# A hybrid decoder layer on one core: the weight sum of a Strassen product made by VectorE, and the order of the merge gate's tiles and the output projection's products changed

## The chip, the cores and the metric

The kernel runs on one NeuronCore of a Trainium2 chip. The engines are TensorE (PE: matmuls; PEld: its weight loads), VectorE (DVE), ScalarE (ACT), GpSimd (POOL) and SyncE (SP), each with its own instruction queue, worked off in order; sixteen DMA engines carry the transfers that SP, ScalarE and GpSimd issue. The metric is device time in microseconds, the median of the runs.

## The reference

The layer has 256 positions and a model width of 1024, all in float32. Cut to what matters here:

```python
h = rmsnorm(x, norm_g) * (1 + scale) + shift            # adaLN: scale, shift, gate from c
proj = h @ w_in                                         # 1024 -> 10 blocks of 1024 columns
q, k, v, g_attn, cb, cc, cx, g_conv, m_attn, m_conv = split(proj)
attn = moba_attention(q, k, v, rel_bias)                # one block of 256 keys: causal softmax
y_attn = (attn * silu(g_attn)) @ w_o_attn
y_conv = (cb * conv3(cc * cx) * silu(g_conv)) @ w_o_conv
merged = sigmoid(m_attn) * y_attn + sigmoid(m_conv) * y_conv
out = rmsnorm(x + gate * (merged @ w_out), final_g)
```

In the kernel's names `ga` and `gc` are the SiLU gates, `ma` and `mc` the sigmoid merge gates of the attention and the convolution branch, `oa` and `oc` the branches' projections (w_o_attn, w_o_conv), and `wo` the output projection (w_out).

## The kernel before, in words

**Precision.** A float32 product is made of three matmuls in a faster format: each operand is split into a high part (ScalarE copies it to the format, line 74) and a low part (VectorE subtracts the high part from the operand, line 75), and high × high, high × low and low × high are summed. So each 1 MB unit of weights costs one 128x2048 instruction on ScalarE and one on VectorE. The names end in `h` and `l`: `ma11l` is the low part of merge gate `ma`, column half 1, contraction half 1.

**Tiles.** `tile(blk, n, kh)` (line 623) loads 512 columns by 512 contraction rows, splits them and issues 24 matmuls of 512 columns, twelve for each of two groups of 128 positions. After `kh` = 1 the result goes through a sigmoid into `SA` (`ma`) or is multiplied into `SA` (`oa`).

**Seven products.** `mc` and `oc` are computed by a Strassen scheme (class `Seven`, line 535). The weights of a block are four quarters (r, c), r the contraction half, c the column half, 1 MB each. Seven products of 12 matmuls replace eight. Three of them, p7, p6 and p4, use a running sum of quarters, `self.sum`: (1,2) + (2,2) for p7, then + (1,1) for p6, then + (2,1) for p4. `begin` (line 542) copies (1,2) into it by a transfer from SP's queue and adds (2,2) by a transfer that adds to what is in memory (`add_on`, line 508, issued by GpSimd); p7 and p6 each start the next addition in the same way, once their operand has been read. p5 uses another sum, `self.first`. p2 and p3 load (2,1) and (2,2) by themselves. The left operands of p7, p5, p6 and p3 are combinations of the activations, made by `combos` (line 511). Partial results wait in three PSUM banks A, B and C; `sink` passes the four result quarters on: for `mc` a sigmoid into `SC` (line 616), for `oc` a multiplication into `SC` (line 619).

**What sets the order.** The code is written in program order, and a tile framework schedules it: each engine's order need not be the written one, and waits are placed by it. Buffers limit how far things run ahead: five raw weight buffers, so a load is issued when the low part of an earlier unit has been made; three buffers each for high and low parts, so a split waits for the matmuls of the third unit before it; and one slot named `W2` which holds first the broadcast condition `csb` for the adaLN gate rows, then `mc`'s sum, then `oc`'s sum, then `gf` (the output gate `gb` and `final_g`).

**From the gates to the end.** Lines 635 to 673 write the order: `ga`'s units with mc's p7, p5, p1 and p6 between them, then the `ma` tiles, mc's p2, p4 and p3, the begin of `oc`, its products and the `oa` tiles. Line 678 transposes the output gate's column into a row, which goes to DRAM and comes back broadcast over all partitions as `gb` (lines 682 and 683). `joined(n)` adds SA and SC for column half n, `turned(n)` transposes the merged half into `M` on TensorE, and the output projection `ao` follows: with `o00` and `o01` for columns 0 to 511, with `o10` and `o11` for the rest. The last quarter of the output gate is multiplied into the raw weights of o10 and o11 (line 699). Then come the residual, the final norm and the output.

Of the kernel before, what the change touches and what calls it, by code (L numbers as in the profile page):

```python
# [35 lines left out]
UNIT = {key: i for i, key in enumerate(UNITS)}  # L36
# [3 lines left out]
def layer_kernel(ctx: ExitStack, tc, x, c, vec, wp_all, slab_all, onehot, final_g, out):  # L40
    nc = tc.nc
# [450 lines left out]
    def gated(blk, src, dst, j):  # L492
        g = unit((blk, j), H, tmp("cc", f"{blk}{j}"))
        sg = tmp("y", f"s{blk}{j}")
        nc.scalar.activation(sg, g, AF.Silu)
        nc.vector.tensor_mul(sg, sg, src[:, 2 * j:2 * j + 2, :])
        put(sg, dst, j)

    def rows_tile(blk, n, kh, xs, a):
        raw = load((blk, n, kh), f"w{blk}{n}{kh}").rearrange("p (k n) -> p k n", k=4)  # L500
        hi, lo = split(raw, [P, 4, 512], f"{blk}{n}{kh}")
        for t in range(2):
            rows_mm(a[t], xs, t, hi, lo, 4 * kh, slice(0, 512), kh == 0, kh == 1)

    def pair(blk, n):
        return [bank(f"a{blk}{n}{t}") for t in range(2)]

    def add_on(t, key):
        nc.gpsimd.dma_start(t, wp_all[UNIT[key]], accum_op=ALU.add)  # L509

    def combos(x, name):
        f = raw_tile([P, 2048], "f" + name).rearrange("p (k n) -> p k n", k=KT)
        nc.vector.tensor_add(f, x[:, :, 0:S].bitcast(F32), x[:, :, S:].bitcast(F32))
        out = {}

        def quarter(t, kh):
            return f[:, 4 * kh:4 * kh + 4, t * P:(t + 1) * P]

        def combo(i, op, a, b, tag):
            v = tp.tile([P, 4, P], F32, tag=tag, name=f"v{name}{i}", bufs=2)  # L520
            op(v, a, b)
            dst = homes[i // 3][:, i % 2]
            nc.scalar.activation(dst[:, :, 0:P], v, AF.Copy)
            nc.vector.tensor_sub(dst[:, :, P:], v, dst[:, :, 0:P].bitcast(F32))
            out[i] = dst
            return v

        homes = [big.tile([P, 2, 4, S], F32R, tag=tag, name=f"sx{name}{tag}") for tag in ("V", "BI")]
        v1 = combo(1, nc.vector.tensor_sub, quarter(1, 0), quarter(1, 1), "cx")
        combo(0, nc.vector.tensor_sub, quarter(0, 0), quarter(1, 0), "cc")  # L530
        v2 = combo(3, nc.vector.tensor_sub, v1, quarter(0, 0), "y")
        combo(4, nc.vector.tensor_add, v2, quarter(0, 1), "cx")
        return {3: out[0], 1: out[1], 2: out[3], 4: out[4]}

    class Seven:
# [5 lines left out]

        def begin(self):
            self.sum = big.tile([P, 2048], F32, tag="W2", name=self.blk + "sum")
            nc.sync.dma_start(self.sum, wp_all[UNIT[self.key(1, 2)]])
            add_on(self.sum, self.key(2, 2))

        def begin_first(self):
# [40 lines left out]

        def p6(self):
            self.product(self.b, self.sum, "p6", False, s=2)  # L590
            add_on(self.sum, self.key(2, 1))
            u3 = self.quad("u3")
            nc.vector.tensor_add(u3, self.b, self.q1)
            nc.vector.tensor_sub(self.q7, u3, self.q7)
            nc.vector.tensor_sub(u3, self.c, u3)
            self.sink(1, 1, u3)

        def p2(self):
            self.product(self.a, self.load(2, 1), "p2", False, t=0, kh=1)
            self.sink(0, 0, self.a)  # L600

        def p4(self):
            self.product(self.b, self.sum, "p4", False, t=1, kh=1)
            nc.vector.tensor_add(self.q1, self.b, self.q1)
            self.sink(1, 0, self.q1)
# [6 lines left out]
    def part(x, t, n):  # L612
        return x[:, t, 512 * n:512 * (n + 1)]
# [9 lines left out]
    def tile(blk, n, kh):  # L623
        if kh == 0:
            banks[blk] = pair(blk, n)
        a = banks[blk]
        rows_tile(blk, n, kh, GA if blk == "oa" else H, a)
        if kh and blk == "ma":
            for t in range(2):
                nc.scalar.activation(part(SA, t, n), a[t], AF.Sigmoid)  # L630
        elif kh:
            for t in range(2):
                nc.vector.tensor_mul(part(SA, t, n), part(SA, t, n), a[t])

    mc, oc = Seven("mc", H, to_gate), Seven("oc", GC, to_merge)
# [17 lines left out]
    mc.p6()  # L653
    gated("ga", AT, GA, 3)
    SA = big.tile([P, 2, D], F32, tag="AT", name="SA")
    tile("ma", 0, 0)
    mc.p2()
    mc.p4()
    tile("ma", 0, 1)
    mc.p3()  # L660
    oc.begin()
    oc.sx = combos(GC, "c")
    tile("ma", 1, 0)
    oc.begin_first()
    tile("ma", 1, 1)
    oc.p7()
    tile("oa", 0, 0)
    oc.p5()
    oc.p1()
    tile("oa", 0, 1)  # L670
    oc.p6()
    oc.p2()
    tile("oa", 1, 0)
    oc.p4()
    gf = big.tile([P, 2 * D], F32, tag="W2", name="gf")
    gb, fg = gf[:, 0:D], gf[:, D:]
# [8 lines left out]
    def joined(n, ts=range(2)):  # L685
        for t in ts:
            nc.vector.tensor_add(part(SA, t, n), part(SA, t, n), part(SC, t, n))

    joined(0)
    oc.p3()  # L690
    M = big.tile([P, KT, 512], F32R, tag="H", name="M")
    wo = {}
# [8 lines left out]

    MR = SA

# [159 lines left out]
```

## Time and profile before

| | |
|---|---|
| median of 3 runs | 326.34 us (326.1 to 326.67) |
| the profiled execution's own time | 326.11 us |
| its span, first to last instruction | 324.2 us |
| TensorE busy | 309.9 us, 96% of the span |
| VectorE busy | 261.1 us, 81% |
| ScalarE busy | 199.3 us, 61% |
| mean granted TensorE clock | 0.992 |
| HBM read | 81.87 MB |

A group or timeline row reads: line, engine, operation, written tile <- read tiles, shape, count. In the timeline the first number is the start in us from the span's start, the second the length; brackets give the idle time of the engine just before and what ended it. A row of stages (A:B) gives length, busy time and number of instructions of PE, PEld, DVE, ACT and POOL, the granted clock, the DMA engines' busy share and GB/s. A DMA row ends with KB each and microseconds from issue to landing. SPq, ACTq and POOLq are the engines' queues. Lengths of neighbouring instructions overlap a little, so steps are better read from start to start.

### The profile page before, as it was taken

To read this page: it belongs to the slowest core of one execution; us is meant where nothing else is said; L and a number is where in the kernel's file an instruction comes from. 1 tells how busy PE (TensorE), PEld (TensorE's weight loads), DVE (VectorE), ACT (ScalarE), POOL (GpSimd) and SP (SyncE) were. 2 spreads that over 40 slices of the span, in tenths; PEclk is the share of its full clock that TensorE was granted. 3 is DMA by queue.
4 is the path that set the end of the run, shared out by engine and by line. 5 is a ranking of instruction groups with operands and counts; after the bars stand their busy time and mean duration, and the time that the engine had idled before them with its cause. 6 is when DMAs were issued, how large, how long until landed. Compare 5 with 4: busy or idle time off the path is not lost.

```text
span 324.2 us, 4594 instructions
## 1 busy us (share of the span) xinstructions
PE 309.9 (96%) x1766; PEld 271.6 (84%) x1766; DVE 261.1 (81%) x365; ACT 199.3 (61%) x292; POOL 15.4 (5%) x25
## 2 busy tenths in 40 slices
PE   7899999999999999999999999999989999599992
PEld 6799999888889988988898888888868888377892
DVE  4899995957699899796978978899757673999774
ACT  2655565763697876676778776779568552722430
POOL 3400000000000000110000100101101010000010
PEclk9999999999999999999999999999999999979999
DMA  7999999996664765997454697738999999250003
GB/s 279 416 409 408 407 418 413 400 351 263 253 236 171 241 281 184 355 213 288 129 210 174 162 293 298 162 129 288 257 327 361 359 394 325 87 196 1 0 2 129
DMA packets 15627, 83.23 MB, mean 257 GB/s; under 512 B 1670, under 2 KB 3062, under 8 KB 8182
## 3 DMA queue, kind: packets, MB, share of 16 engines
q1 hardware_dynamic: 12816, 72.49, 57.0%
q0 software_dynamic: 1184, 8.40, 13.1%
q10 hardware_dynamic: 1606, 2.05, 1.9%
q8 instruction: 14, 0.23, 0.3%
q14 instruction: 7, 0.06, 0.0%
HBM read 81.87 MB, written 1.06 MB: 256 GB/s over the span
## 4 chain that ended last, share of the span: by engine, by line
PE 73%; DVE 11%; DMA 9%; ACT 3%; issue 3%; POOL 0%; POOLq 0%; SPq 0%; ACTq 0%; DVEq 0%
PE acc L202 14%; PE agc L346 5%; PE acc L346 5%; PE acx L346 5%; PE acb L346 5%; DMA ocsum<-in_wp_dram 4%; DMA wma<-in_wp_dram 4%; PE aga L346 3%; PE acb L348 2%; PE agc L348 2%; PE acx L348 2%; PE acc L348 2%; PE av L362 2%; PE av L363 2%; PE av L361 2%
## 5 line engine op out<-in xcount | busy, mean ns | idle before, releaser
L509 POOL DMA_DIRECT2D mcsum<-in_wp_dram x3 | 2.6, 881 | 182.9 <-PE pS L413 119.7
L387 DVE CUSTOM_DVE_ANT_0 gate<-gate,wide,vT 128x1024 f32<-128x1024 f32 x8 | 10.2, 1279 | 0.0
L165 DVE CUSTOM_DVE_ANT_0 ada<-ada,wide,msc 128x1024 f32<-128x1024 f32 x7 | 9.4, 1341 | 0.0
L165 DVE CUSTOM_DVE_ANT_0 ada<-ada,wide,vT 128x1024 f32<-128x1024 f32 x7 | 8.9, 1277 | 0.0
L332 ACT ACTIVATE lowcb<-acb 128x256 f32<-128x256 f32 x8 | 3.0, 374 | 6.5 <-PE acb L348 6.5
L75 DVE TENSOR_TENSOR ma11l<-wma,ma11h 128x2048 fp32r<-128x2048 f32 x1 | 2.3, 2293 | 5.7 <-ACT ma11h L74 5.7
L353 ACT ACTIVATE M<-pm 128x512 fp32r<-128x512 f32 x4 | 2.2, 597 | 7.4 <-PE pm L710 7.4
L75 DVE TENSOR_TENSOR ocp4l<-ocsum,ocp4h 128x2048 fp32r<-128x2048 f32 x1 | 2.3, 2292 | 5.5 <-ACT ocp4h L74 5.5
L737 ACT ACTIVATE SQ<-TT 128x512 f32<-128x512 f32 x3 | 1.9, 627 | 7.1 <-DVE TT L732 7.1
L74 ACT ACTIVATE ocp4h<-ocsum 128x2048 fp32r<-128x2048 f32 x1 | 1.9, 1917 | 6.4 <-DMA ocsum<-in_wp_dram 6.4
L380 ACT ACTIVATE V<-av 128x512 f32<-128x512 f32 x4 | 2.4, 598 | 5.1 <-PE av L363 5.1
L75 DVE TENSOR_TENSOR cb0l<-wcb,cb0h 128x2048 fp32r<-128x2048 f32 x1 | 2.3, 2292 | 3.6 <-ACT cb0h L74 3.6
L74 ACT ACTIVATE ma11h<-wma 128x2048 fp32r<-128x2048 f32 x1 | 1.9, 1918 | 4.7 <-DMA wma<-in_wp_dram 4.7
L477 ACT ACTIVATE y<-cc,vT 128x256 f32<-128x256 f32 x8 | 3.9, 504 | 1.4 <-DVE cc L473 1.4
L332 ACT ACTIVATE lowcx<-acx 128x256 f32<-128x256 f32 x8 | 3.0, 376 | 2.9 <-PE acx L348 2.8
L143 PE MATMUL wt<-ones 128*128 128x128 f32 x18 | 3.8, 381 | 1.0 <-DVE ones L131 1.0
L333 DVE TENSOR_TENSOR cc<-acc,lowcc 128x256 f32<-128x256 f32 x8 | 3.4, 421 | 1.7 <-ACT lowcc L332 1.7
L74 ACT ACTIVATE o01h<-wo 128x2048 fp32r<-128x2048 f32 x1 | 1.9, 1917 | 4.3 <-PE ocC L560 4.3
L202 PE MATMUL acc<-hf,slab 128*128 128x256 f32 x16 | 3.9, 386 | 0.7 <-ACT hf L261 0.7
L362 PE MATMUL ama<-ma11l,H 128*128 128x512 f32 x8 | 3.2, 404 | 1.3 <-DVE ma11l L75 1.3
L75 DVE TENSOR_TENSOR oa01l<-woa,oa01h 128x2048 fp32r<-128x2048 f32 x1 | 2.3, 2291 | 2.7 <-ACT oa01h L74 2.7
L403 DVE TENSOR_TENSOR AX<-QK,AX 128x384 fp32r<-128x384 f32 x8 | 4.4, 551 | 0.0
(552 smaller groups left out, 1149.0 us busy)
## 6 DMA issues: line engine op xcount, KB each, us to landing
ada<-in_wp_dram SPq DMA_DIRECT2D x16, 512.0 KB, 10.2
slab<-in_slab_dram SPq DMA_DIRECT2D x16, 512.0 KB, 10.2
wv<-in_wp_dram SPq DMA_DIRECT2D x4, 1024.0 KB, 11.3
wcc<-in_wp_dram SPq DMA_DIRECT2D x4, 1024.0 KB, 4.8
wcx<-in_wp_dram SPq DMA_DIRECT2D x4, 1024.0 KB, 5.0
gate<-in_wp_dram SPq DMA_DIRECT2D x4, 1024.0 KB, 7.3
wcb<-in_wp_dram SPq DMA_DIRECT2D x4, 1024.0 KB, 6.6
wgc<-in_wp_dram SPq DMA_DIRECT2D x4, 1024.0 KB, 8.3
```

What stands on the lines that cost most here:

```text
L74: pin(nc.scalar.activation(hi[:, s], raw[:, s], AF.Copy))
L75: pin(nc.vector.tensor_sub(lo[:, s], raw[:, s], hi[:, s].bitcast(F32)))
L165: pin(nc.vector.tensor_tensor_reduce(src, src, csb, vT[:, i:i + 1] if s else 1.0, bias(i, s), ALU.mult, ALU.add, scs[:, i, s:s + 1]))
L202: pin(nc.tensor.matmul(acc[j // 2][:, (j % 2) * S:(j % 2 + 1) * S], w[i][:, j * P:(j + 1) * P], x, start=(i == 0 and j // 2 not in opened) ...
L332: nc.scalar.activation(low, a[:, S:], AF.Copy)
L346: nc.tensor.matmul(a, hi[:, k, cols], rhs[:, k, :], start=(k == 0), stop=False)
L348: nc.tensor.matmul(a[:, S:], lo[:, k, cols], rhs[:, k, 0:S], start=False, stop=(k == KT - 1))
L361: nc.tensor.matmul(a, xh, hi[:, k4, cols], start=(first and k4 == 0), stop=False)
L362: nc.tensor.matmul(a, xh, lo[:, k4, cols], start=False, stop=False)
L363: nc.tensor.matmul(a, xl, hi[:, k4, cols], start=False, stop=(last and k4 == 3))
L387: nc.vector.tensor_tensor_reduce(src, src, csb, 1.0, vT[:, 24 + d:25 + d], ALU.mult, ALU.add, gcol[:, d:d + 1])
L403: nc.vector.tensor_sub(lo, src, hi.bitcast(F32))
```

## The change

The third addition to the sum is no longer a transfer: p2 keeps the quarter (2,1) that it loads, and at the head of p4 VectorE adds it to the sum. The copy in `begin` is issued by GpSimd, not by SP. And the written order changes: mc's p2 stands ahead of tile ma00, oc's `begin` ahead of tile ma01, p7 ahead of tile ma11, p5 ahead of oa00, p6 ahead of oa01, p2 and p4 behind oa01, and tile oa10 behind `joined(0)`.

```diff
         def begin(self):
             self.sum = big.tile([P, 2048], F32, tag="W2", name=self.blk + "sum")
-            nc.sync.dma_start(self.sum, wp_all[UNIT[self.key(1, 2)]])
+            nc.gpsimd.dma_start(self.sum, wp_all[UNIT[self.key(1, 2)]])
             add_on(self.sum, self.key(2, 2))
...
         def p6(self):
             self.product(self.b, self.sum, "p6", False, s=2)
-            add_on(self.sum, self.key(2, 1))
             u3 = self.quad("u3")
...
         def p2(self):
-            self.product(self.a, self.load(2, 1), "p2", False, t=0, kh=1)
+            self.w21 = self.load(2, 1)
+            self.product(self.a, self.w21, "p2", False, t=0, kh=1)
             self.sink(0, 0, self.a)
 
         def p4(self):
+            nc.vector.tensor_add(self.sum, self.sum, self.w21)
             self.product(self.b, self.sum, "p4", False, t=1, kh=1)
...
     SA = big.tile([P, 2, D], F32, tag="AT", name="SA")
+    mc.p2()
     tile("ma", 0, 0)
-    mc.p2()
     mc.p4()
+    oc.begin()
     tile("ma", 0, 1)
     mc.p3()
-    oc.begin()
     oc.sx = combos(GC, "c")
     tile("ma", 1, 0)
     oc.begin_first()
+    oc.p7()
     tile("ma", 1, 1)
-    oc.p7()
+    oc.p5()
     tile("oa", 0, 0)
-    oc.p5()
     oc.p1()
+    oc.p6()
     tile("oa", 0, 1)
-    oc.p6()
     oc.p2()
-    tile("oa", 1, 0)
     oc.p4()
...
     joined(0)
+    tile("oa", 1, 0)
     oc.p3()
```

Line numbers behind line 602 grow by one in the changed kernel (L604 to L605, L699 to L700).

VectorE's order where the gate units end, the changed kernel against the one before (`mcsum` and `wmc_2253` are mc's sum and its quarter (2,1), `ga3l` the low part of the last gate unit):

```order
 L333 TENSOR_TENSOR ga_2106<-aga_2113,lowga_2130 128x256
-L75 TENSOR_TENSOR ga3l<-wga_2202,ga3h 128x2048
+L603 TENSOR_TENSOR mcsum<-mcsum,wmc_2253 128x2048
 L354 TENSOR_TENSOR GA<-sga_2084,GA 128x2x256
 L333 TENSOR_TENSOR ga_2106<-aga_2133,lowga_2150 128x256
+L75 TENSOR_TENSOR ga3l<-wga_2201,ga3h 128x2048
```

The new addition stands where ga3l stood; ga3l follows two small instructions later.

ScalarE's order at the end of the merge gate's tiles, before and then changed (`ocp7h` is the high part of oc's sum for p7, `sxcBI` combinations of activations):

```order
L74 ACTIVATE ma10h<-wma_2400 128x2048
L630 ACTIVATE SA<-ama_2254 128x512
L630 ACTIVATE SA<-ama_2255 128x512
L74 ACTIVATE ma11h<-wma_2433 128x2048
L523 ACTIVATE sxcBI<-vc_2390 128x4x128
L523 ACTIVATE sxcBI<-vc_2394 128x4x128
L74 ACTIVATE ocp7h<-ocsum 128x2048
```

```order
L631 ACTIVATE SA<-ama_2273 128x512
L74 ACTIVATE ocp7h<-ocsum 128x2048
L523 ACTIVATE sxcBI<-vc_2390 128x4x128
L523 ACTIVATE sxcBI<-vc_2394 128x4x128
L74 ACTIVATE ma11h<-wma_2453 128x2048
L617 ACTIVATE SC<-mcq_2034 128x512
```

The split of oc's sum for p7 stood behind that of ma11; now it stands ahead of it. VectorE's low parts are in the same order.

VectorE's order where the attention tiles end and the output projection begins, before and then changed (`wo_2810` is the raw weight of o11, `gf` holds gb):

```order
L75 TENSOR_TENSOR oa11l<-woa_2723,oa11h 128x2048
L604 TENSOR_TENSOR ocq_2553<-ocB,ocq_2553 128x512
L75 TENSOR_TENSOR o00l<-wo_2757,o00h 128x2048
L619 TENSOR_TENSOR SC<-SC,ocq_2553 128x512
L609 TENSOR_TENSOR ocq_2482<-ocC,ocq_2482 128x512
L687 TENSOR_TENSOR SA<-SA,SC 128x512
L619 TENSOR_TENSOR SC<-SC,ocq_2482 128x512
L633 TENSOR_TENSOR SA<-SA,aoa_2628 128x512
L75 TENSOR_TENSOR o01l<-wo_2763,o01h 128x2048
```

```order
L75 TENSOR_TENSOR oa11l<-woa_2723,oa11h 128x2048
L687 TENSOR_TENSOR SA<-SA,SC 128x512
L700 TENSOR_TENSOR wo_2810<-wo_2810,gf 128x4x256
L610 TENSOR_TENSOR ocq_2450<-ocC,ocq_2450 128x512
L75 TENSOR_TENSOR o00l<-wo_2757,o00h 128x2048
L620 TENSOR_TENSOR SC<-SC,ocq_2450 128x512
L354 TENSOR_TENSOR M<-pm_2709,M 128x2x256
L354 TENSOR_TENSOR M<-pm_2716,M 128x2x256
L634 TENSOR_TENSOR SA<-SA,aoa_2656 128x512
L75 TENSOR_TENSOR o01l<-wo_2763,o01h 128x2048
```

The gate's multiplication into o11's weights, which stood behind the merge of the second column half, now stands ahead of o00l and of M's low parts.

## The prediction

> All times below are microseconds from the start of the profiled execution; "ends" and "starts" of the changed kernel are worked out, not measured.
>
> **What bounds the kernel now.** I read the page's first part, then the chain of work that ended last, then TensorE's timeline from 210 on, where the change begins to act.
>
> ```profile
> span 324.2 us, 4594 instructions
> PE 309.9 (96%) x1766; PEld 271.6 (84%) x1766; DVE 261.1 (81%) x365; ACT 199.3 (61%) x292; POOL 15.4 (5%) x25
> ```
>
> TensorE sets the end: it is busy 96% of the span, and what an edit can win is what TensorE still waits. In the timeline (start, length, instruction, and in brackets the idle time before it):
>
> ```profile
> 215.24 0.40 PE L361 MATMUL ama<-ma00h,H 128*128 128x512 f32 x1
> 220.70 0.39 PE L560 MATMUL mcA<-mcp2h,H 128*128 128x512 f32 x1
> 223.42 0.39 PE L560 MATMUL mcB<-mcp4h,H 128*128 128x512 f32 x1
> ...
> 241.43 0.50 PE L362 MATMUL ama<-ma11l,H 128*128 128x512 f32 x1 [1.29 <-DVE ma11l L75]
> 278.67 0.50 PE L560 MATMUL ocB<-ocp4l,GC 128*128 128x512 f32 x1 [1.59 <-DVE ocp4l L75]
> 283.87 0.50 PE L560 MATMUL ocC<-ocp3l,sxcBI 128*128 128x512 f32 x1 [2.08 <-DVE ocp3l L75]
> ...
> 294.28 0.39 PE L363 MATMUL aoa<-oa11h,GA 128*128 128x512 f32 x1
> 294.84 0.50 PE L361 MATMUL ao<-o00h,M 128*128 128x512 f32 x1 [0.17 <-DVE M L354]
> 301.34 0.39 PE L361 MATMUL ao<-o01h,M 128*128 128x512 f32 x1
> ```
>
> A gate or attention tile (24 matmuls) takes 220.70 − 215.24 = 5.46, a Strassen product (12) 223.42 − 220.70 = 2.72. From 215.24 to the end of the attention tiles stand eight tiles, ten products and 0.9 of transposes: 43.7 + 27.2 + 0.9 = 71.8, so without a wait they would end at 287.0. The last matmul starts at 294.28 and with a step of 0.23 ends at 294.5. So **7.5 are lost in this stretch**. Where, the chain of waits and the stages say:
>
> ```profile
> 225.22 11.82 DMA wma<-in_wp_dram
> 237.13 1.93 ACT ma11h L74
> ...
> 262.39 11.87 DMA ocsum<-in_wp_dram
> 274.37 1.93 ACT ocp4h L74
> ```
>
> ```profile
> 205.00:210.00 5.00, 5.00 (x24) 4.13 (x23) 4.55 (x4) 4.05 (x7) 0.00 (x0) 1.00 1.00 188
> 240.00:245.00 5.00, 3.71 (x17) 2.97 (x17) 5.00 (x5) 3.89 (x4) 0.00 (x0) 1.00 1.00 423
> 285.00:290.00 5.00, 5.00 (x18) 3.91 (x17) 5.00 (x6) 1.92 (x1) 0.00 (x0) 0.66 0.70 271
> ```
>
> The load of ma11 lands 11.8 after its issue; the third addition to ocsum (quarter (2,1)) is issued only when p6's low part is made and lands 11.9 later, and p4 and, behind it on VectorE, p3's low part wait for it. The idle brackets make 1.29 + 1.59 + 2.08 = 5.0. In 285:290 the granted clock is 0.66 (the third number from the end, ahead of DMA share and GB/s), right behind the two long waits: 5 × 0.34 = 1.7. The 0.8 that is left lies beside the brackets (the first matmul after each takes 0.50, not 0.39).
>
> **The additions by transfer, and the queue they run on.** Issue times on GpSimd's queue, and KB and time to landing of single transfers:
>
> ```profile
> 203.44 0.86 POOL L509 DMA_DIRECT2D mcsum<-in_wp_dram  x1 [19.04 <-DVE mcp6l L75]
> 227.78 0.87 POOL L509 DMA_DIRECT2D ocsum<-in_wp_dram  x1 [2.89 <-DVE vc L521]
> 245.74 0.86 POOL L509 DMA_DIRECT2D ocsum<-in_wp_dram  x1 [17.09 <-DVE ocp7l L75]
> ```
>
> ```profile
> mcsum<-in_wp_dram POOLq DMA_DIRECT2D x1, 1024.0 KB, 8.1
> ocsum<-in_wp_dram SPq DMA_DIRECT2D x1, 1024.0 KB, 6.0
> ocsum<-in_wp_dram POOLq DMA_DIRECT2D x1, 1024.0 KB, 13.3
> ocsum<-in_wp_dram POOLq DMA_DIRECT2D x1, 1024.0 KB, 10.9
> ```
>
> The one at 203.44 runs alone: 8.1. At 227.78, behind another addition in its queue and beside loads: 13.3. At 245.74, beside loads only: 10.9. The stages say why: an addition alone fills all 16 engines at 188 GB/s, loads alone reach 423 GB/s, so an addition costs the engines over twice its bytes.
>
> **Removed: (2,1) by transfer, once in mc, once in oc.** p4's operand is then made by a VectorE addition from the quarter that p2 loads anyway. In oc this takes the 11.87 out of the path: the 1.59 and 2.08 and the slow clock behind them go.
>
> **Added: two VectorE additions of 128x2048.** No row is this instruction; the nearest is the sum of two f32 tiles of the same size, fc at L513:
>
> ```profile
> 203.66 0.42 DVE L333 TENSOR_TENSOR ga<-aga,lowga 128x256 f32<-128x256 f32 x1
> 208.60 2.28 DVE L513 TENSOR_TENSOR fc<-GC 128x2048 f32<-128x2048 f32 x1
> 210.80 0.69 DVE L496 TENSOR_TENSOR sga<-sga,AT 128x512 f32<-128x512 f32 x1
> 211.40 0.68 DVE L593 TENSOR_TENSOR mcu<-mcB,mcq 128x512 f32<-128x512 f32 x1
> 212.00 2.28 DVE L75 TENSOR_TENSOR ma00l<-wma,ma00h 128x2048 fp32r<-128x2048 f32 x1
> 214.20 0.69 DVE L354 TENSOR_TENSOR GA<-sga,GA 128x512 fp32r<-128x512 f32 x1
> ...
> 218.87 2.28 DVE L75 TENSOR_TENSOR mcp4l<-mcsum,mcp4h 128x2048 fp32r<-128x2048 f32 x1
> ```
>
> From start to start that is 2.2 for 2048 columns and 0.60 for 512. Below nothing it can't be; above 2.3 no row of this size lies. In mc it stands behind the row at 203.66, where VectorE now waits for ga3h until 205.45, so 1.4 of its 2.2 fill an idle gap, and what follows shifts. Laying the new order end to end with these steps: mc's addition 204.0–206.2, ga3l done 209.3 (its first use, 8 matmuls into ga3, is at 211.5), mcp2l 212.8 (use 215.5), ma00l 217.1 (use 218.2), **mcp4l 219.3** (use 223.7), ma01l 224.1 (use 226.4), ma10l 232.9 (use 234.5). All in time, the closest by 1.1, so here TensorE runs on, and the addition costs nothing. In oc it stands between ocp6l and oa01l, with p2, p4, oa tiles in a new order; laid out the same way oa01l is done 1.5 before its use. Cover gone, each would cost up to 2.2.
>
> **Moved: oc's begin.** Now SP's copy is issued at 221.2 behind mcp4l; the changed kernel has GpSimd issue it behind mcp4l at 219.6 (0.3 after it, as at 245.74). No row shows a plain 1 MB copy from GpSimd: bounds are SP's 6.0 and the lone addition's 8.1; an addition holds the engines 2.9 longer than a load (1.05 MB at 188 against 423 GB/s: 5.6 − 2.5 = 3.1), so 8.1 − 3 = 5.1 would be the lowest. I take 5.5, nearest to SP's row: landed 225.1. The addition of (2,2) is issued at 225.6 (0.5 after a landing: 221.2 + 6.0 against 227.78). Its bounds are 8.1 and 13.3. The load of woa00 runs beside it from about 229, the addition to oct comes behind it instead of ahead, so the row at 245.74 is its likeness: 10.9, landed 236.5.
>
> And here the new order costs. p7 now stands *ahead* of tile ma11, so it has its turn at 239.74, not 246.8. ocp7h (ScalarE, 1.93) and ocp7l (2.2) then end at 240.8; the second matmul of p7 wants ocp7l at 239.97. ma11h stands behind ocp7h on ScalarE, and ma11l behind ocp7l and three 512-wide instructions on VectorE: 236.5 + 1.95 + 2.2 + 1.8 + 2.2 = 244.65, while TensorE without a wait wants it at 242.7. **The new wait is s = 2.0**, in two pieces of about 1 each. With the landing between 233.7 (8.1) and 238.9 (13.3) s lies between 0 and 4.4. What follows (p5, oa00, p1, p6, oa01, p2, p4, oa10, p3) has its low parts ready in that layout, the closest by 0.9, oa10l. So the attention tiles end at 287.0 + s = 289.0.
>
> [...]
>
> **Moved along with it: the output gate's row.** On VectorE the gain on wo11 (L699 before, L700 after) now stands right behind oa11l and the merge, *ahead of* p3's last combination, o00l, M's low parts and o01l. It waits for gb, which comes through DRAM by two transfers of ScalarE's queue:
>
> ```profile
> 283.59 0.30 ACTq L682 DMA_DIRECT2D gd<-grow  x1
> 287.89 0.35 ACTq L683 DMA_DIRECT2D gf<-gd  x1
> 297.10 1.22 DVE L699 TENSOR_TENSOR wo<-wo,gf 128x1024 f32<-128x1024 f32 x1
> ```
>
> ```profile
> gf<-gd ACTq DMA_DIRECT2D x1, 512.0 KB, 4.4
> out_dram<-TT ACTq DMA_DIRECT2D x2, 192.0 KB, 2.7
> out_dram<-TT SPq DMA_DIRECT2D x2, 320.0 KB, 2.5
> ```
>
> Before, it runs at 297.10 and waits for neither. Now: oa11h waits for p4's end (272.4 + s), the row is issued at 274.8 + s, lands after about 2.6 (nearest rows out_dram's 2.7 and 2.5; bounds 0 and the 4.3 between the two issues), the broadcast lands 0.3 + 4.4 later: 282.1 + s. VectorE is free for it at 279.1 + s, so it stands still for 3.0. From the gb landing VectorE needs 1.15 + 0.6 + 2.2 + 0.6 + 0.6 to M's first low part (5.15 later) and 10.1 to the first merged half of columns 512 to 1023, for which turned(1)'s transposes wait. The projection's tiles start where TensorE is nearly free anyway, but turned(1) stops it for about 1.4, and o01 starts 13.1 to 13.3 behind the landing: at 295.3 + s, against 301.34 now. Of TensorE's own work it could start at 293.0 + s.
>
> **The sum.** From o01 on both kernels do the same; o10l now has a multiplication for ao0 ahead of it, but is done in time. So the gain is 301.34 − 295.3 − s = 6.0 − 2.0 = 4.0 (7.5 lost before are won, 2.0 come back at p7 and ma11, about 1.5 more than before around the projection's start). The profiled execution took 326.11 (its span and 1.9 around it), 0.23 less than the median of the runs, 326.34: 326.34 − 4.0 = 322.3, and as the new pieces lean on unmeasured landings I say **322.4**.
>
> **The rivals.**
> 1. *The chain is in time.* If (2,2) lands by 234.3 (8.7 after its issue, 8.1 is on record), s is 0: 320.4. For it: oct's addition no longer runs ahead. Against: 13.3, 10.9 and 11.87 all stand with loads beside them. Chance 0.20.
> 2. *The gate's row is unseen.* If gd lands at once and the broadcast in less than 4.4, VectorE goes on at 279.1 + s and o01 starts at 293.0 + s, 2.3 earlier: 320.1 at s = 2.0, partly hidden more likely 321. Against: 2.5 to 2.7 is the quickest landing in DRAM among these rows. Chance 0.10.
> 3. *VectorE becomes the bound in the gate tiles.* It is full from 205.45 to 233, and the least slack is 1.1 (ma00l). Two instructions of 0.6 that fall late ahead of ma00l, or another 1.2, and TensorE waits; the later mcp4l pushes begin by as much and s with it: 1 to 2 in all, 323.5 to 324.5. Chance 0.10.
> 4. *The pair of transfers lands late, and the kernel is slower.* If VectorE's instructions can hold up what GpSimd issues, the copy issued at 219.6 starts only after fc and ma01l, 2 × 2.2 later, s is 6.4, and p7's wait in one piece of over 4 brings the 0.66 clock back (1.7): 6.0 − 6.4 − 1.7 = −2.1, 328.4. It decides from a landing about 2.5 to 4 later than my 236.5, that is from 239 to 240.5. Against: the addition at 203.44, issued amid VectorE work (the stage's 4.55 of 5), lands in 8.1. The same end comes if copy and addition both take the worst seen. Chance 0.08. [...]
> 5. *Nothing comes of it*: s of 4 and a late gb together, within 0.65 of before. Chance 0.04.
>
> **How the numbers follow.** My own case has the remaining 0.48, with s from 1.0 to 3.5: 321.3 to 323.8. The bounds of s (0 to 4.4) give 320.3 to 324.7, those of gb 0.7 either way; leaving out the slower case and half of the fastest corner, the range is 319.6 to 325.2. About 0.2%, 0.65, is what a measurement of this kernel tells from no change. Faster: 0.48 + 0.20 + 0.10 + 0.10 less some tail, 0.86; same 0.05; slower 0.09.
>
> **What would show it.** In the changed profile: idle brackets before ocp7l and ma11l of about 1 each and ocp7h released by the ocsum transfer at 236 to 237; none before ocp4l and ocp3l, and no stage with a clock of 0.66; VectorE idle about 3 before L700, released by gf; a wait before pm of turned(1) of about 1.4; o01 at about 297. I am wrong if ocp7h starts after 239, if ma00l, ma01l or ma10l gets a bracket, or if TensorE waits for ocp5l, oa01l or oa10l.

## The result, and the profile after

The changed kernel takes 322.55 us (median of 4 executions, 321.16 to 323.54) against 326.5 for the kernel before: a ratio of 0.9877, with a 95% interval from 0.9834 to 0.9921. A second series of six executions gives 322.47 (322.12 to 324.08), ratio 0.9884 (0.9866 to 0.9903). The forecast was 322.4, range 319.6 to 325.2.

The profiled execution took 323.24. Its page and TensorE's timeline:

```profile
span 321.3 us, 4588 instructions
PE 308.2 (96%) x1766; PEld 270.3 (84%) x1766; DVE 264.9 (82%) x367; ACT 199.6 (62%) x292; POOL 13.8 (4%) x25
```

```profile
242.09 0.50 PE L560 MATMUL ocB<-ocp7l,sxcV 128*128 128x512 f32 x1 [1.44 <-DVE ocp7l L75]
246.10 0.50 PE L362 MATMUL ama<-ma11l,H 128*128 128x512 f32 x1 [0.95 <-DVE ma11l L75]
...
290.57 0.47 PE L361 MATMUL ao<-o00h,M 128*128 128x512 f32 x1
...
295.14 0.44 PE L711 MATMUL pm<-ident,SA 128*128 128x128 f32 x2 [0.90 <-DVE SA L687]
...
298.28 0.39 PE L361 MATMUL ao<-o01h,M 128*128 128x512 f32 x1
```

The brackets at ocp4l and ocp3l are gone. In their place stand two, at ocp7l and at ma11l, and one at the transposes `pm` of turned(1). Tile o01 starts at 298.28, not 301.34. Of the lead, 0.5 is lost before this stage: the first matmul on `hf` starts at 11.92 here and at 11.39 in the profile before, in code that is the same in both; over all the runs of this study it moves between 11.1 and 12.1.

What released the engines at these places (ScalarE and VectorE), a stage and the transfers of the chain (the last number is from issue to landing):

```profile
237.80 1.92 ACT L74 ACTIVATE ocp7h<-ocsum 128x2048 fp32r<-128x2048 f32 x1 [4.90 <-DMA ocsum<-in_wp_dram]
245.22 1.91 ACT L74 ACTIVATE ocp5h<-oct 128x2048 fp32r<-128x2048 f32 x1 [1.91 <-DMA oct<-in_wp_dram]
285.26 1.23 DVE L700 TENSOR_TENSOR wo<-wo,gf 128x1024 f32<-128x1024 f32 x1 [2.60 <-DMA gf<-gd]
```

```profile
285.00:290.00 5.00, 5.00 (x25) 4.17 (x24) 4.74 (x5) 2.33 (x3) 0.00 (x0) 1.00 0.00 0
```

```profile
wma<-in_wp_dram SPq DMA_DIRECT2D x1, 1024.0 KB, 6.2
ocsum<-in_wp_dram POOLq DMA_DIRECT2D x1, 1024.0 KB, 12.1
oct<-in_wp_dram POOLq DMA_DIRECT2D x1, 1024.0 KB, 18.9
```

The addition of (2,2) is issued at 225.63 and lands 12.1 later, at 237.7. The addition to oct stands 0.56 behind it in GpSimd's queue and lands at 245.1. The load of ma11 is issued at 224.64, 1.0 ahead of the two, and lands in 6.2 instead of 11.8: the wait that ma11 had before is cured, and ma11l is late for another reason, its place behind ocp7h and ocp7l.

### The profile page after: what moved, and what is told of

It is laid out like the page before. It is cut to its first block, busy times and chain, and to the rows that moved or that the text cites. A ratio compares the mean times of both kernels' runs of the same rounds, so it can differ in the third digit from the quotient of the medians.

```text
span 321.3 us, 4588 instructions
## 1 busy us (share of the span) xinstructions
PE 308.2 (96%) x1766; PEld 270.3 (84%) x1766; DVE 264.9 (82%) x367; ACT 199.6 (62%) x292; POOL 13.8 (4%) x25
## 3 DMA queue, kind: packets, MB, share of 16 engines
HBM read 79.77 MB, written 1.06 MB: 252 GB/s over the span
## 4 chain that ended last, share of the span: by engine, by line
PE 69%; DVE 12%; DMA 8%; issue 5%; ACT 3%; POOL 1%; SPq 0%; POOLq 0%; ACTq 0%; DVEq 0%
PE acc L202 15%; PE agc L346 5%; PE acc L346 5%; PE acx L346 5%; PE acb L346 5%; DMA ocsum<-in_wp_dram 4%; PE acx L348 2%; PE agc L348 2%; PE acb L348 2%; PE acc L348 2%; PE aga L346 2%; PE av L361 2%; PE av L363 2%; PE av L362 2%; DMA xx<-in_x_dram 2%
## 5 line engine op out<-in xcount | busy, mean ns | idle before, releaser
L75 DVE TENSOR_TENSOR ocp7l<-ocsum,ocp7h 128x2048 fp32r<-128x2048 f32 x1 | 2.3, 2291 | 4.9 <-ACT ocp7h L74 4.9
L544 POOL DMA_DIRECT2D mcsum<-in_wp_dram x1 | 0.6, 582 | 112.6 <-DVE cc L333 112.6
L74 ACT ACTIVATE ocp7h<-ocsum 128x2048 fp32r<-128x2048 f32 x1 | 1.9, 1917 | 4.9 <-DMA ocsum<-in_wp_dram 4.9
L756 POOL TENSOR_TENSOR rf<-ms,mhalf 128x1 f32<-128x1 f32 x2 | 1.7, 834 | 72.1 <-DVE ms L783 68.7
L700 DVE TENSOR_TENSOR wo<-wo,gf 128x1024 f32<-128x1024 f32 x2 | 2.4, 1220 | 2.6 <-DMA gf<-gd 2.6
L312 DVE TENSOR_SCALAR QK<-acc 128x512 f32<-128x512 f32 x2 | 1.4, 689 | 3.8 <-PE acc L202 3.8
L169 ACT ACTIVATE H<-xnT,scs 128x256 fp32r<-128x256 f32 x7 | 4.1, 588 | 0.3 <-DVE scs L165 0.3
L74 ACT ACTIVATE o00h<-wo 128x2048 fp32r<-128x2048 f32 x1 | 1.9, 1918 | 3.8 <-PE aoa L363 3.8
```

Source lines behind the costliest of these rows:

```text
L75: pin(nc.vector.tensor_sub(lo[:, s], raw[:, s], hi[:, s].bitcast(F32)))
L169: pin(nc.scalar.activation(dst, xnT[:, i, :], AF.Identity, scale=scs[:, i, 1:2], bias=scs[:, i, 0:1]))
```

## The experiments

The prediction rests on a sum: the third transfer's wait won, s paid at p7 and ma11, about 1.5 paid for the output gate's row. The first four runs ask for the two prices. The rival to each is that the wait is hidden or moves on.

**The changed kernel again**, as the yardstick.

> The changed kernel once more, as the yardstick on the same chip for the three below. Both theories: 322.5 within 1, with TensorE's two idle brackets at ocp7l (about 1.4) and ma11l (about 1.0) and VectorE's idle of about 2.6 before the gain of the gate on wo11 (L700).

Measured: 322.47. In its profile (2,2) lands at 236.9 and the two brackets are 0.63 and 0.99; o01 starts at 297.16, 1.1 earlier than in the first. So s moves with the landing of one transfer: 2.39 in the first profile, 1.62 in this one, which is 0.77 of the 1.12 between the two profiled executions. What spreads the other executions no trace shows.

**The gate's row early.** The transpose, the copy and the transfer to DRAM go up to where the gate tiles end:

```diff
     gated("ga", AT, GA, 3)
+    pgt = bank("pgt")
+    nc.tensor.transpose(pgt[0:KT, 0:P], gcol, ident)
...
+    nc.scalar.dma_start(gd, grow)
     SA = big.tile([P, 2, D], F32, tag="AT", name="SA")
...
     gf = big.tile([P, 2 * D], F32, tag="W2", name="gf")
     gb, fg = gf[:, 0:D], gf[:, D:]
-    pgt = bank("pgt")
-    nc.tensor.transpose(pgt[0:KT, 0:P], gcol, ident)
...
-    nc.scalar.dma_start(gd, grow)
     nc.scalar.dma_start(gb, bass.AP(tensor=gd.tensor, offset=gd.offset, ap=[[0, P], [1, D]]))
```

> The changed kernel with the gate's transpose, its copy grow and its transfer gd written ahead of the merge's buffers, so that the transfer gf<-gd is issued earlier by one tile or more and VectorE need not stand still for it. Theory (the row's wait costs at the projection's start, about 1.5 of the forecast's sum): the idle of 2.6 before L700 goes, the start of tile o01 comes 1.5 to 2.3 earlier, the time is 320.3 to 321.0, that is 1.5 to 2.2 below the changed kernel of the same chip. Rival (VectorE's idle is hidden behind the matmuls of the last tiles): the idle goes, o01 and the time stay within 0.5 of the changed kernel.

Measured: 320.06 (318.89 to 321.56), ratio 0.9809 (0.9786 to 0.9832), which lies clear of the changed kernel's interval: 2.4 less, a little more than the 1.5 to 2.2 that the theory gave. TensorE and VectorE at the projection:

```profile
290.44 0.39 PE L361 MATMUL ao<-o00h,M 128*128 128x512 f32 x1
...
293.16 1.03 PE L711 MATMUL pm<-ident,SA 128*128 128x128 f32 x8
...
296.78 0.39 PE L361 MATMUL ao<-o01h,M 128*128 128x512 f32 x1
```

```profile
292.72 1.21 DVE L700 TENSOR_TENSOR wo<-wo,gf 128x1024 f32<-128x1024 f32 x1
```

The bracket before `pm` is gone, the row L700 stands late and waits for nothing. From o00's start to o01's are 296.78 − 290.44 = 6.34, against 298.28 − 290.57 = 7.71 in the changed kernel (7.45 in its second profile). So 1.1 to 1.4 of the 2.4 are shown at this place. The rest lies within the spread of the executions (the profiled one, 321.56, is the upper end of its range); what it is stays open.

**Tile ma11 ahead of p7 again.**

```diff
     oc.begin_first()
-    oc.p7()
     tile("ma", 1, 1)
+    oc.p7()
     oc.p5()
```

> The changed kernel with one move taken back: tile ma11 stands ahead of the product p7 again. Theory (p7 comes before its addition has landed, s = 2): ma11l's and ocp7l's brackets of 0.95 and 1.44 go or shrink below 0.5 together, since p7's turn is then one tile, 5.5, later than the landing at about 237.7 needs; the time is 320.0 to 321.0, about 2 below the changed kernel. Rival (the loads of wma, as before at L362 ma11l, are late by themselves): a bracket of 1 or more stays before ma11l and the time falls by less than 1.

Measured: 321.46 (320.82 to 324.69), ratio 0.9861 (0.983 to 0.9892), 1.0 below the yardstick, and by itself not told apart from it. TensorE and ScalarE:

```profile
249.27 0.50 PE L560 MATMUL ocC<-ocp5l,sxcV 128*128 128x512 f32 x1 [0.60 <-DVE ocp5l L75]
```

```profile
244.98 1.92 ACT L74 ACTIVATE ocp5h<-oct 128x2048 fp32r<-128x2048 f32 x1 [5.01 <-DMA oct<-in_wp_dram]
```

Both brackets went, as the theory has it, but the gain is about half of the 2 expected. Of what is missing, 0.60 shows: p5 stands right behind p7, and oct, second in GpSimd's queue, lands at 245.0, too late for p5.

**Both edits.**

> The two edits together: gate's row early and ma11 ahead of p7. If the two waits are separate losses in line on TensorE's path, the gains add up: 3.5 to 4.2 below the changed kernel, 318.3 to 319.0, and no bracket of 0.5 or more stands on TensorE between 205 and the projection. If they overlap (VectorE's lateness is carried from the one place to the other), the sum is smaller: 320.0 to 320.5.

Measured: 319.07 (318.55 to 319.52), ratio 0.977 (0.9756 to 0.9785), the fastest kernel of the study and with the smallest spread of those that beat the kernel before. The gains add up: 2.4 + 1.0 = 3.4, and 322.47 − 319.07 = 3.4. No bracket of 0.3 or more stands on TensorE from 205 to the projection. In this execution oct lands at 244.0, 1.0 earlier than in the run before, and p5 does not wait. Tile o01 starts here:

```profile
294.20 0.39 PE L361 MATMUL ao<-o01h,M 128*128 128x512 f32 x1
```

The gate's row is a loss of its own, behind that of p7.

So the two prices together, 3.4, are as forecast (2.0 + 1.5), and the kernel without them lies 326.58 − 319.07 = 7.5 below the kernel before, which is what the forecast counted as won. The next runs ask whether the gain is what the forecast said: VectorE's sum alone, the new order alone, the issuer alone.

**VectorE's sum alone**, in the kernel before: SP's copy and the old order stay.

```diff
         def p6(self):
...
-            add_on(self.sum, self.key(2, 1))
...
         def p2(self):
-            self.product(self.a, self.load(2, 1), "p2", False, t=0, kh=1)
+            self.w21 = self.load(2, 1)
+            self.product(self.a, self.w21, "p2", False, t=0, kh=1)
...
         def p4(self):
+            nc.vector.tensor_add(self.sum, self.sum, self.w21)
```

> The kernel before with one part of the change alone: VectorE adds quarter (2,1) from the load of p2, in mc and in oc; the order of tiles and products, and SP's copy, stay as before. Theory (the third addition by transfer is what was lost, and the two sums on VectorE are free): the brackets at ocp4l (1.59) and ocp3l (2.08) and the stage at clock 0.66 go, 1.59 + 2.08 + 1.7 + about 0.4 beside the brackets = 5.8; the wait for ma11l (about 1.3) stays, and the gate's row stands late, unseen: 320.5 to 321.5, so faster than the whole change (322.5). Rival (the new order is what pays, since without it p4's sum has only one product of cover behind p2 and lands on the path): a bracket of 1 or more before ocp4l or ocp3l stays, 323.5 or more.

Measured: 326.97 (326.15 to 327.5), ratio 1.0013 (1.0002 to 1.0025): nothing is gained, and the rival's reason is wrong too, since no bracket stands at ocp4l or ocp3l. TensorE, a stage, SP's queue and one transfer:

```profile
242.34 0.50 PE L361 MATMUL ama<-ma11h,H 128*128 128x512 f32 x1 [2.11 <-ACT ma11h L74]
244.67 0.79 PE L362 MATMUL ama<-ma11l,H 128*128 128x512 f32 x1 [1.82 <-DVE ma11l L75]
...
294.43 0.50 PE L361 MATMUL ao<-o00h,M 128*128 128x512 f32 x1 [0.96 <-DVE M L354]
```

```profile
245.00:250.00 5.00, 5.00 (x17) 4.01 (x17) 5.00 (x4) 3.16 (x3) 0.87 (x1) 0.73 0.99 419
```

```profile
219.68 0.33 SPq L544 DMA_DIRECT2D ocsum<-in_wp_dram  x1
220.06 0.42 SPq L65 DMA_DIRECT2D wma<-in_wp_dram  x1
220.53 0.43 SPq L65 DMA_DIRECT2D oct<-in_wp_dram  x1
...
226.22 0.33 SPq L65 DMA_DIRECT2D wma<-in_wp_dram  x1
```

```profile
wma<-in_wp_dram SPq DMA_DIRECT2D x1, 1024.0 KB, 14.1
```

The scheduler now puts SP's copy ahead of the loads of ma10 and oct. It waits for mcp4l until 219.68, and the two loads behind it go out only then (in the changed kernel at 213.37 and 217.74). The load of ma11 goes out at 226.22, 1.3 behind the addition of (2,2), and takes 14.1. The wait at ma11 grows from 1.29 to 2.11 + 1.82, the clock behind it costs 5 × 0.27 = 1.35 in this stage alone, and M is waited for by 0.96. What p4 wins, ma11 gives back.

**The new order alone**: the changed kernel with the third addition by transfer and SP's copy.

```diff
         def begin(self):
-            nc.gpsimd.dma_start(self.sum, wp_all[UNIT[self.key(1, 2)]])
+            nc.sync.dma_start(self.sum, wp_all[UNIT[self.key(1, 2)]])
...
         def p6(self):
...
+            add_on(self.sum, self.key(2, 1))
...
         def p4(self):
-            nc.vector.tensor_add(self.sum, self.sum, self.w21)
```

> The changed kernel with the third addition by transfer again, in mc and in oc, and SP's copy; only the new order is left of the change. Theory of the forecast (the chain through the third transfer is the loss, a VectorE sum its cure): p4's turn in the new order is near 269 to 272, p6's low part is made near 258, and a transfer issued then lands at 267 to 270 (8 to 12 later), so ocp4l is made at 271 to 274: one bracket of 0 to 3 is left at ocp4l, no clock stage; with the waits at p7 and the gate's row, 322.5 to 325.5. Rival (the new order alone hides the transfer, and the sum adds nothing to it): no bracket at ocp4l and 322 to 323, the same as the changed kernel.

Measured: 333.99 (333.63 to 334.67), ratio 1.0231 (1.0212 to 1.025). Both theories missed by 8 and more. TensorE, two stages and GpSimd's queue:

```profile
246.70 0.79 PE L560 MATMUL ocB<-ocp7h,sxcV 128*128 128x512 f32 x1 [6.22 <-ACT ocp7h L74]
249.03 0.79 PE L560 MATMUL ocB<-ocp7l,sxcV 128*128 128x512 f32 x1 [1.53 <-DVE ocp7l L75]
...
286.28 0.50 PE L362 MATMUL aoa<-oa10l,GA 128*128 128x512 f32 x1 [1.43 <-DVE oa10l L75]
```

```profile
245.00:250.00 5.00, 1.77 (x3) 1.12 (x4) 3.32 (x3) 4.88 (x5) 0.73 (x1) 0.50 0.39 165
250.00:255.00 5.00, 5.00 (x13) 3.88 (x12) 5.00 (x4) 2.92 (x4) 0.13 (x1) 0.50 0.88 157
```

```profile
224.51 0.86 POOL L509 DMA_DIRECT2D oct<-in_wp_dram  x1 [19.78 <-DVE sga L496]
228.56 0.87 POOL L509 DMA_DIRECT2D ocsum<-in_wp_dram  x1 [3.18 <-DMA ocsum<-in_wp_dram]
```

Here oct's addition goes ahead of (2,2) in GpSimd's queue, as in the kernel before, and (2,2) lands at 244.7. In the old order p7 has its turn behind ma11 and can afford such a landing (241.1 in the kernel before, and no bracket at p7). In the new one it stands ahead of ma11: 6.22 + 1.53 of waiting, and a granted clock of 0.50 in both stages. The queue's order, which no line of the edit names, is what differs beside the edit itself; no bracket stands at ocp4l, whose transfer came back with the edit.

**SP's copy in the changed kernel** (only the line in `begin` goes back).

> The changed kernel with the first copy of the chain issued by SP again, as before, ahead of GpSimd's addition. Theory (the copy's landing, 5.0 from GpSimd and 6.0 from SP, passes on to (2,2), p7 and the end): (2,2) lands 0.5 to 1.5 later, ocp7l's and ma11l's brackets grow by as much together, 322.5 to 324. Rival (the issuer doesn't matter): within 0.5 of the changed kernel.

Measured: 323.07 (322.68 to 323.81), ratio 0.9899 (0.9883 to 0.9915): 0.6 above the yardstick, with overlapping intervals. (2,2) lands at 238.3, the brackets are 1.72 and 0.39. SP's copy holds the loads here too: ma11's is issued at 224.86 and lands at 240.1, as late as with the sum alone. But ma11 now has its turn behind p7, and its bracket is only 0.39. With both sums and the new order in place the issuer hardly counts.

**The fastest kernel with mc's third addition as a transfer again**: in `p6` and `p4` the two lines depend on the block.

```diff
         def p6(self):
...
+            if self.blk == "mc":
+                add_on(self.sum, self.key(2, 1))
...
         def p4(self):
-            nc.vector.tensor_add(self.sum, self.sum, self.w21)
+            if self.blk == "oc":
+                nc.vector.tensor_add(self.sum, self.sum, self.w21)
```

> The version with the gate's row early and ma11 ahead of p7, in which mc's third quarter is added by transfer again, as in the kernel before (oc's stays on VectorE). It also puts oct's addition ahead of ocsum's (2,2) in GpSimd's queue. Theory (mc's sum was never on the path, on either engine, and only landings in oc count): no bracket in the gate tiles at 205 to 225; (2,2) lands 12 to 13.5 after its issue, 1 to 2.5 later than with oct behind it, while p7's second matmul wants its operand at 245.8, that is a landing by 241.6, so this is hidden, and oct's own landing, earlier by 3 or more, is hidden too: 318.7 to 319.5, the same. Rival (taking mc's transfer away freed the engines for the loads beside it, and so was part of the gain): 320 or more, with brackets at ma00l, mcp2l or mcp4l.

Measured: 322.82 (322.05 to 324.61), ratio 0.989 (0.9867 to 0.9913), 3.8 above the version with both sums. The profiled execution, 324.61, is the upper end of the range. TensorE and GpSimd's queue:

```profile
240.27 0.50 PE L361 MATMUL ama<-ma11h,H 128*128 128x512 f32 x1 [0.32 <-ACT ma11h L74]
242.59 0.50 PE L362 MATMUL ama<-ma11l,H 128*128 128x512 f32 x1 [1.82 <-DVE ma11l L75]
263.51 0.50 PE L560 MATMUL ocB<-ocp6l,sxcBI 128*128 128x512 f32 x1 [1.58 <-DVE ocp6l L75]
268.04 0.50 PE L362 MATMUL aoa<-oa01l,GA 128*128 128x512 f32 x1 [1.51 <-DVE oa01l L75]
```

```profile
221.57 0.57 POOL L544 DMA_DIRECT2D ocsum<-in_wp_dram  x1 [17.43 <-ACT sga L495]
223.94 0.86 POOL L509 DMA_DIRECT2D oct<-in_wp_dram  x1 [1.80 <-issue]
227.50 0.86 POOL L509 DMA_DIRECT2D ocsum<-in_wp_dram  x1 [2.70 <-DMA ocsum<-in_wp_dram]
246.84 0.86 POOL L509 DMA_DIRECT2D ocsum<-in_wp_dram  x1 [18.48 <-DVE ocp7l L75]
```

Neither theory holds whole. Nothing in the gate tiles waits for mc's transfer (no bracket between 205 and 240), so much is as the theory says. But VectorE's order changes with it, mcp4l comes at 218.73 instead of 217.44, the copy is issued at 221.57 instead of 220.03, and oct's addition now goes out ahead of (2,2) and of ma11's load (225.65, landing after 12.6). p7 is in time, as expected. But ma11's load lands at 238.3, and ma11 waits 0.32 + 1.82 for it. And the addition of (1,1) behind p7 is issued at 246.84, not 241.29, lands at 259.1, and p6 waits 1.58 and oa01 1.51. Two links beside and behind p7 were late, which the expectation had not followed.

**The sum with GpSimd's copy, the copy alone, and the new order with GpSimd's copy** complete the table of the three parts of the change. The edits are those shown above, made in the kernel before (the third in the changed one).

> The kernel before with VectorE's sum (mc and oc) and GpSimd's copy at the head of the chain, the order of tiles and products as before. Theory formed from the run of the sum alone (there SP's copy of ocsum stood in SP's queue ahead of the loads of ma10 and oct until mcp4l was made, 219.68, all loads behind it went out beside the additions, and wma of ma11 landed at 240.3): with the copy on GpSimd's queue wma is issued near 224.5 and lands near 231, the brackets at ma11 go, p7 stands behind ma11 and finds (2,2) landed at 237 to 238: 319.5 to 321, below the whole change. Rival (the order is needed, the loads are late with either issuer): 324 or more, with a bracket at ma11 again.

> The kernel before with GpSimd's copy alone; the third addition stays a transfer, the order as before. Theory: the copy lands about 1 earlier, but oct's addition still stands ahead of (2,2) in GpSimd's queue and the third addition still ends p4's wait: the brackets at ocp4l and ocp3l stay, 325 to 326.5, within 1.5 of before. Rival (the issuer of the copy is what pays): 323 or less.

> The changed kernel without VectorE's sums: the new order and GpSimd's copy, the third addition by transfer. In GpSimd's queue oct's addition stands ahead of (2,2) here, as in the run of the order alone. Theory (p7 ahead of ma11 needs (2,2) by 236, and behind oct's addition it lands 12 to 16 after 227.5, at 240 to 244): a wait of 3 to 6 before p7, part of it paid a second time by a clock of 0.5 to 0.7, no bracket at ocp4l: 327 to 333, slower than before. Rival (SP's copy was what made the order alone slow): 322 to 324.

| VectorE's sums | GpSimd's copy | new order | median us | ratio (95%) |
|---|---|---|---|---|
| no | yes | no | 326.55 | 1.0007 (0.9995 to 1.0019) |
| yes | no | no | 326.97 | 1.0013 (1.0002 to 1.0025) |
| yes | yes | no | 321.83 | 0.9863 (0.9839 to 0.9888) |
| no | no | yes | 333.99 | 1.0231 (1.0212 to 1.025) |
| no | yes | yes | 336.3 | 1.0304 (1.0289 to 1.0319) |
| yes | no | yes | 323.07 | 0.9899 (0.9883 to 0.9915) |
| yes | yes | yes | 322.47 | 0.9884 (0.9866 to 0.9903) |

The sum and GpSimd's copy together, without the new order, give 321.83, a little above the 319.5 to 321 expected, and cannot be told from the whole change. In the profiled execution, at 320.38 the lower end of its range (to 323.26), only one bracket is left on TensorE:

```profile
288.21 0.50 PE L361 MATMUL ao<-o00h,M 128*128 128x512 f32 x1 [0.95 <-DVE M L354]
```

The copy alone brings nothing: its brackets are 1.64 at ma11l (the row below), 1.48 at ocp4l, 2.08 at ocp3l, 0.38 at the transposes and 1.04 at M. The new order without the sum is slower with either issuer: with GpSimd's copy (2,2) lands at 246.0 and the wait before p7 is 7.46 + 1.53, and its 336.3 lies above the 327 to 333 that were expected. Here GpSimd's copy costs 2.3 against SP's; with the sum and the old order it wins 326.97 − 321.83 = 5.1.

```profile
242.24 0.50 PE L362 MATMUL ama<-ma11l,H 128*128 128x512 f32 x1 [1.64 <-DVE ma11l L75]
```

**The queue's order by itself.** In every kernel with both sums GpSimd adds (2,2) ahead of oct, in every other one behind it. So the last run takes the copy alone and writes oct's load behind ma11's:

```diff
-    oc.begin_first()
     tile("ma", 1, 1)
+    oc.begin_first()
```

> The kernel before with GpSimd's copy, and oct's load and addition written behind tile ma11, so that SP loads wma ahead of oct and GpSimd adds (2,2) ahead of oct; no sum on VectorE, TensorE's order as before. All four kernels with the sums on VectorE in both projections and the early chain have this queue order, all without them the other; this run separates the two. Theory 1 (the sum's gain is the third transfer that p4 no longer waits for; the queue order is worth only the wait at ma11, 1.64 in the run of the copy alone): ma11's bracket goes, ocp4l's and ocp3l's 1.5 and 2.1 stay, 324 to 325.3. Theory 2 (the queue order is what pays): the brackets at ocp4l and ocp3l shrink too, since the whole chain of additions starts earlier, 321.5 to 323, like the sum and the copy together.

Measured: 325.18 (324.32 to 325.63), ratio 0.9955 (0.9943 to 0.9968). TensorE, and GpSimd's queue:

```profile
276.94 0.50 PE L560 MATMUL ocB<-ocp4l,GC 128*128 128x512 f32 x1 [1.71 <-DVE ocp4l L75]
282.15 0.50 PE L560 MATMUL ocC<-ocp3l,sxcBI 128*128 128x512 f32 x1 [2.07 <-DVE ocp3l L75]
...
292.96 0.50 PE L361 MATMUL ao<-o00h,M 128*128 128x512 f32 x1 [1.04 <-DVE M L354]
```

```profile
227.23 0.86 POOL L509 DMA_DIRECT2D ocsum<-in_wp_dram  x1 [5.22 <-DMA ocsum<-in_wp_dram]
230.31 0.86 POOL L509 DMA_DIRECT2D oct<-in_wp_dram  x1 [2.22 <-DVE sxcV L524]
```

The bracket at ma11l is gone and 326.55 − 325.18 = 1.4 is gained; ocp4l and ocp3l wait as ever. Theory 1 holds: the order of the queues is worth the wait at ma11, the sum the wait at p4 and p3. Which queue it is stays open: the edit also moves ma11's load ahead of oct's in SP's queue, and it goes out at 218.41 instead of 225.69 in the run of the copy alone, so the order of GpSimd's additions is not tried by itself. From here to the kernel with sum and copy are 325.18 − 321.83 = 3.35, about the two brackets.

## Why the prediction was right, and where it was not

The time came out within 0.2 us, and so did the sum behind it: 7.5 won, 3.5 paid, against 7.5 and 3.4. That it is as near as 0.2 is in part luck, since four executions of the changed kernel spread over 2.4. What the forecast did not see is on what some of the pieces hang.

1. *7.5 us lost before, all won.* The version without the two prices is 7.5 faster than the kernel before, so the whole was there to be won, but not by the sum alone. The pieces 1.59 and 2.08 hang on the sum: 3.35 between the last run and the kernel with sum and copy. The piece at ma11, 1.29, hangs on the order of the queues (1.4); the forecast counted it as won without saying why ma11's load should land in time. The 1.7 of slow clock hid another wait. Two kernels with brackets of the same size at ocp4l and ocp3l, the copy alone and the oct-late one, have a granted clock of 1.00 from 270 to 292.5, and the first of them takes 326.55 all the same: in them TensorE waits 1.04 for M, where the kernel before waited 0.17. With the sum and the copy in the old order 0.95 of that wait is left; in the new order there is no bracket at M.
2. *The two sums are free.* On VectorE they are, as the forecast laid out: 2.28 each, and no bracket at ma00l, ma01l, ma10l or oa01l. The least slack in the gate tiles is ma00l's, 1.06, where the forecast had 1.1. The forecast had mcp4l earlier and (2,2) ahead of oct in GpSimd's queue too, but did not ask which edit brings them. Both hang on mc's sum: where it goes back to a transfer, in the fastest kernel, both are lost, and that costs 3.8.
3. *The copy on GpSimd, landed 5.5 after its issue.* It took 5.2 (220.17 to 225.4). (The lower bound beside it is worked out with 2.9, then with 3.1; 8.1 − 3.1 = 5.0, and nothing in the sum changes.) The forecast read the move as an earlier landing alone. In the kernels with the sum it also takes a copy that waits for mcp4l out of SP's in-order queue, where it stands ahead of two loads (in the sum alone it goes out at 219.68, the loads at 220.06 and 220.53). In the old order this is worth 5.1, more than any single wait that the forecast counted; in the changed kernel itself it is worth 0.6, which cannot be told from nothing.
4. *s = 2.0 at p7 and ma11.* The landing forecast for 236.5 came at 237.7 and 236.9. The brackets are 1.44 + 0.95 and 0.63 + 0.99: s is 1.6 to 2.4. What follows has its low parts ready, as forecast, the closest oa10l by 1.02 (forecast 0.9). That holds for the changed kernel only: with ma11 first, p5 comes sooner and waits 0.60 for oct, and the time falls by 1.0, not by 2.
5. *The gate's row, about 1.5.* VectorE stands still for 2.60 (forecast 3.0), TensorE waits 0.90 before `pm` (forecast 1.4), and undoing it shortens the projection's start by 1.1 to 1.4 and the time by 2.4. Rival 2, that the row is unseen, falls.
6. *The new order.* The forecast priced two of its waits and took it for neutral otherwise. With the sum and GpSimd's copy in place it is worth nothing that can be measured (321.83 without it, 322.47 with it). Without its two waits it is worth 321.83 − 319.07 = 2.8 between the medians and 320.38 − 319.07 = 1.3 between the profiled executions, of which 0.95 is the wait for M; the rest is not assigned.

Of the other rivals, the first (the chain in time) wanted (2,2) by 234.3 and falls, and the third (VectorE full in the gate tiles) shows no bracket. The fourth is what happens to the new order without the sum: the pair lands late, p7 pays for it and the clock falls. It put a wait of s = 6.4, over 4 of it at p7, and 1.7 of slow clock on a landing 4.4 later than forecast; the landing at 244.7, 8.2 later, costs 6.22 + 1.53 of waiting and two stages at 0.50. Its cause is not the one named, that VectorE's instructions hold up GpSimd's issue: in the changed kernel GpSimd issues the copy at 220.17, while VectorE runs `fc` from 220.13, and it lands in 5.2.

## What to carry to other kernels

Price a moved transfer by what stands behind it in its queue and by what it then runs beside, not by its own landing: the same 1 MB load took between 5.1 and 15.2 here, by what else was in flight. When a scheduler orders the queues, compare them for every part of an edit; taking back one sum on VectorE turned round two additions in GpSimd's queue. And when a late wait is cured, follow every operand of the next two or three steps to its landing: in two runs here the next one was late in its turn (0.60 at p5, 1.58 at p6).

## What the runs showed of the hardware

The same 1 MB load, that of ma11 through SP's queue, landed after very different times: 6.2 when it was issued 1.0 ahead of the first addition with the copy nearly landed (the changed kernel; 5.1 in its second profile, issued at the same place); 9.0 when issued 0.5 behind the addition (the sum with GpSimd's copy); 10.4 ahead of oct's addition by 0.7, but with SP's copy still under way (the order alone); 11.8 and 12.6 behind oct's addition by 1.2 and 1.7 (the kernel before, mc's transfer); 14.1 and 15.2 with two held-back loads and an addition beside it (the sum alone, SP's copy). So by these seven loads in flight count too, not only additions; no rule from the place of one alone fits all seven. In the changed kernel the second of two additions issued within 0.6 lands 7.4 behind the first (237.7 and 245.1), near the 8.1 of the lone one in the kernel before, as if they ran one after the other.

The granted clock fell for whole pieces of time, to 0.50. Stages of 2.5 of the order alone, of the sum alone, and of the kernel before:

```profile
245.00:247.50 2.50, 0.79 (x1) 0.29 (x1) 0.82 (x1) 2.50 (x3) 0.00 (x0) 0.50 0.78 328
252.50:255.00 2.50, 2.50 (x7) 1.91 (x7) 2.50 (x2) 0.88 (x2) 0.00 (x0) 0.50 1.01 210
```

```profile
245.00:247.50 2.50, 2.50 (x7) 1.92 (x7) 2.50 (x3) 2.16 (x2) 0.00 (x0) 0.50 0.99 416
247.50:250.00 2.50, 2.50 (x12) 2.09 (x11) 2.50 (x2) 1.00 (x2) 0.87 (x1) 0.96 1.00 423
```

```profile
285.00:287.50 2.50, 2.50 (x8) 1.92 (x7) 2.50 (x3) 0.00 (x0) 0.00 (x0) 0.53 0.85 341
287.50:290.00 2.50, 2.50 (x11) 1.99 (x10) 2.50 (x4) 1.92 (x1) 0.00 (x0) 0.78 0.55 202
```

In stages of 0.5 of the kernel before the clock is 1.00 or 0.50, with a value between only where it changes (0.67 from 285.0 to 285.5, 0.91 from 288.5 to 289.0); the 0.66 there and the 0.73 of the sum alone are means over longer stages. By the stages it is at 0.50 from 285.17 to 288.59 in the kernel before, from 244.27 to 247.68 in the sum alone and from 244.77 to 255.01 in the order alone: 3.41, 3.41, and 10.24, three times as long. In the kernel before it falls again at 322.72, 34.13 after its return, ten times as long.

A long wait did not always cost clock. TensorE waits 1.59 and 2.08 at ocp4l and ocp3l in the kernel before, 1.48 and 2.08 in the copy alone, 1.71 and 2.07 in the oct-late kernel. In the first the clock falls at 285.17, 1.30 behind the end of the second wait; in the other two it is 1.00 in every stage of 2.5 from 270 to 292.5. What decides between the two no run tried.
